# Seven-product feed-forward units: weight blocks and sums paired in another way, and the second weight chunk loaded into another buffer

## The chip, the core and the metric

One core of a Trainium2 chip runs the whole program, two layers of an encoder in float32. The metric is the device time of one execution in microseconds (us); lower is better. TensorE multiplies, VectorE (DVE) and ScalarE (ACT) do the elementwise work, GpSimd (POOL) does almost nothing here, and SyncE's queue (SP) issues nearly all loads and stores.

## What is computed

Each layer projects the normed input, runs two groups of heads (retention and differential attention), adds the projected result to `x`, and ends with a gated feed-forward part. Only that last part is touched:

```python
h = rms_norm(x, ffn_norm_g[l])
x = x + (jax.nn.silu(h @ w_gate[l]) * (h @ w_up[l])) @ w_down[l]
```

`x` is 512 rows of 1024, `w_gate` and `w_up` are 1024 x 2816, `w_down` is 2816 x 1024, and there are two layers.

## The kernel before, in words

**Precision.** Every float32 operand of a product is split into a high part, rounded to the matmul's float32r type, and a low part, the rest. A product is three matmuls: high x high, high x low, low x high. A split is one ScalarE cast (`hi`) and one VectorE subtraction (`lo`).

**Feed-forward part.** The 2816 inner columns are cut into 22 blocks of 128 (`ff`), taken in four groups: `FFN = [(0, 4), (4, 12), (12, 18), (18, 22)]`. After the blocks of a group, the group's part of the down projection is added to `x`. The first group (`gate_up`) is plain: two products per block, of full depth. The other three groups, 18 blocks a layer and 36 in all, are computed by `seven` (L726 to L773). It takes gate and up together as a 2 x 2 block product: the depth of 1024 is cut in two halves (g1, g2 of the gate weight, u1, u2 of the up weight), the 512 rows of `x` in two halves, and seven products of a Strassen kind stand for eight. The combinations on the side of `x` are made once a layer (`combine`, L695 to L716, during the first group and after it) and stay in memory as high and low parts. On the weights' side each unit makes four sums: s3 = u1 - g1, s1 = u1 - u2, s2 = g1 - s1, s4 = g2 - s2 (L730 to L733, 128 x 512 each).

**A unit's weights.** The host lays them out as two chunks of 128 x 1024: `a` = (g1, u2) and `b` = (g2, u1). Both are loaded into the tag `raw` (three buffers; L727, with the issue in `load_piece`, L168). The sums s31 = (s3, s1) and s24 = (s2, s4) lie in the tag `ah` (three buffers; the attention uses it earlier). `split_in` (L718 to L721) splits `a` into one buffer pair `hi`/`lo`, of which there are three (`NHL`), and `s31` into another one. The same three pairs serve every other weight chunk of the kernel, among them the down projection's (`split_chunk`, L192 and L196). s2 and s4 are split apart into four buffers of the tag `mix` (`split`, L220 and L221), and g2 into two of the tag `rn`; in the last group s24 is split as one into two buffers of tag `h`, and g2 goes to tag `w`.

**A unit's products.** `product` (L747 to L751) issues 12 matmuls of 256 columns: four depth tiles, three matmuls each. In the order of the program: g1 into bank `pa` (tag `acc`), a ScalarE copy of `pa` into `g` (L756); s2 added onto `pa`, copied into `g` (L759); s1 into `pc` (tag `o`); s3 added onto `pa`, copied into `u` (L762) and summed with `pc` on VectorE (L763); g2 into `pb` (tag `sc`), added to `g` (L765); u2 added onto `pa`; then the next unit's preparation and its g1; then s4 added onto `pc`, summed into `g` (L769), the Silu, two multiplications (L771, L772) and the split of the result for the down projection. So s2 waits for the copy of g1's result, s3 for the copy of s2's, u2 for the copy of s3's, and s4 for L763. Each of the three bank tags has two banks.

**Order of the work.** The program's order is a priority, no more: the kernel is written with a tile framework that orders each engine's instructions, when the program is built, by a simulated timeline (`schedule_with_timeline_sim=True`), and hands buffers of a tag to the tiles that ask for them. So the order on an engine departs from the program's where an operand was not ready in that timeline. Once built, each engine runs its list in order; a wait holds what is behind it. The generators `seven` are advanced by L787 to L792: first step (preparation and g1) of a unit, middle step (s2 to u2), first step of the next, last step (s4 and the end).

**Down projection.** Its weight chunks are loaded by L800 into `raw`, split by L192 and L196, multiplied by L203 to L205 (512 columns) and added to `x` by L631.

Of the kernel before, what the change touches and what calls it, by code (L numbers as in the profile page):

```python
# [8 lines left out]
F32 = mybir.dt.float32  # L9
F32R = mybir.dt.float32r  # L10
AF = mybir.ActivationFunctionType
ALU = mybir.AluOpType

P = 128
D = 1024
T = 512
DEPTH = 2
# [5 lines left out]
FT = DFF // P  # L23
# [10 lines left out]
FFN = [(0, 4), (4, 12), (12, 18), (18, FT)]  # L34
PLAIN = FFN[0][1]
# [4 lines left out]
NW, NQK, NMIX, NAH, NHL = 12, 11, 20, 3, 3  # L40
# [14 lines left out]
def encoder_kernel(ctx: ExitStack, tc: tile.TileContext, xT, wfirst, wsingle, wvv, wout, wgu, wdn, prm, lam, cst, outT):  # L55
    nc = tc.nc
# [4 lines left out]
    tpool = ctx.enter_context(tc.tile_pool(name="tpool", bufs=1))  # L61
# [5 lines left out]
    def nm(s):  # L67
        uid[0] += 1
        return f"{s}{uid[0]}"

    def big(s, dt=F32, tag="w", bufs=NW):
        return tpool.tile([P, T], dt, tag=tag, name=nm(s), bufs=bufs)
# [19 lines left out]
    def f32(ap):  # L92
        return ap.bitcast(F32)
# [68 lines left out]
    def new_chunk(n, pieces=1):  # L162
        return wpool.tile([P, 1024], F32, tag="raw", name=nm("raw"), bufs=3), n, pieces

    def load_piece(new, src, i):
        raw, n, pieces = new
        s = slice(i * n // pieces, (i + 1) * n // pieces)
        nc.sync.dma_start(raw[:, s], src[:, s])  # L168

    def load_chunk(src, n=1024, pieces=1):  # L170
        new = new_chunk(n, pieces)
        for i in range(pieces):
            load_piece(new, src, i)
        return new

    def parts():
        return tuple(wpool.tile([P, 1024], F32R, tag=t, name=nm(t), bufs=NHL) for t in ("hi", "lo"))
# [40 lines left out]
    def split(src, tag, bufs):  # L218
        hi, lo = pair() if tag == "h" else [big(n, F32R, tag, bufs) for n in ("hi", "lo")]
        nc.scalar.copy(hi, src)  # L220
        nc.vector.tensor_tensor(lo, src, f32(hi), op=ALU.subtract)  # L221
        return hi, lo
# [84 lines left out]
    def layer(l, n1, h, x_src, first_raw):  # L307
# [28 lines left out]
        mix = [None] * 8  # L336
# [378 lines left out]
                )  # L715
            )  # L716

        def split_in(raw, hi, lo, n=1024):  # L718
            nc.scalar.copy(hi, raw[:, :n])  # L719
            nc.vector.tensor_tensor(lo, raw[:, :n], f32(hi), op=ALU.subtract)  # L720
            return [(hi[:, i * T : (i + 1) * T], lo[:, i * T : (i + 1) * T]) for i in range(n // T)]  # L721

        def wide():
            return tpool.tile([P, 1024], F32R, tag="h", name=nm("s24"), bufs=8)

        def seven(ff, act, tag, bufs):  # L726
            a, b = load_chunk(wgu[l, ff, 0])[0], load_chunk(wgu[l, ff, 1])[0]  # L727
            s31, s24 = (tpool.tile([P, 1024], F32, tag="ah", name=nm("s"), bufs=NAH) for _ in range(2))
            u1 = b[:, T:]
            nc.vector.tensor_tensor(s31[:, :T], u1, a[:, :T], op=ALU.subtract)  # L730
            nc.vector.tensor_tensor(s31[:, T:], u1, a[:, T:], op=ALU.subtract)
            nc.vector.tensor_tensor(s24[:, :T], a[:, :T], s31[:, T:], op=ALU.subtract)
            nc.vector.tensor_tensor(s24[:, T:], b[:, :T], s24[:, :T], op=ALU.subtract)  # L733

            late = ff >= FFN[-1][0]
            g1, u2 = split_in(a, *parts())
            tag2 = ("w", NW) if late else ("rn", 4)
            if late:
                s2, s4 = split_in(s24, wide(), wide())
            else:  # L740
                s2, s4 = (split(s24[:, i * T : (i + 1) * T], "mix", NMIX) for i in range(2))
            s3, s1 = split_in(s31, *parts())
            (g2,) = split_in(b, big("g2h", F32R, *tag2), big("g2l", F32R, *tag2), T)

            pa, pb, pc = (bank() for bank in (acc_bank, sc_bank, out_bank))

            def product(ps, w, r, start):  # L747
                for k in range(4):
                    L, R = cut(w, slice(None), slice(k * P, (k + 1) * P)), comb[k][r]
                    for i, (x1, x2) in enumerate(((0, 0), (0, 1), (1, 0))):  # L750
                        nc.tensor.matmul(ps[:, :C], L[x1], R[x2], start=start and k + i == 0, stop=k == 3 and i == 2, skip_group_check=True)  # L751


            g, u = big("g"), big("u")
            product(pa, g1, "b11", True)
            nc.scalar.copy(g[:, H1], pa[:, :C])  # L756
            yield
            product(pa, s2, "t2", False)
            nc.scalar.copy(g[:, H2], pa[:, :C])  # L759
            product(pc, s1, "t1", True)  # L760
            product(pa, s3, "t3", False)
            nc.scalar.copy(u[:, H2], pa[:, :C])  # L762
            nc.vector.tensor_tensor(u[:, H2], pc[:, :C], u[:, H2], op=ALU.add)  # L763
            product(pb, g2, "b21", True)
            nc.vector.tensor_tensor(g[:, H1], pb[:, :C], g[:, H1], op=ALU.add)  # L765
            product(pa, u2, "t4", False)
            yield
            product(pc, s4, "b22", False)
            nc.vector.tensor_tensor(g[:, H2], pc[:, :C], g[:, H2], op=ALU.add)  # L769
            func(g, g, AF.Silu)  # L770
            nc.vector.tensor_tensor(u[:, H1], pa[:, :C], g[:, H1], op=ALU.mult)  # L771
            nc.vector.tensor_tensor(u[:, H2], u[:, H2], g[:, H2], op=ALU.mult)  # L772
            act.append(split(u, tag, bufs))  # L773

        for a0, a1 in FFN:
# [6 lines left out]
            else:  # L782
                units = []
                for ff in range(a0, a1):
                    tag = ("h", 8) if not last else ("mix", NMIX) if ff < a0 + 2 else ("rn", 4)
# [7 lines left out]
            n = (a1 - a0) * P  # L793
            for m in range(KT):
# [7 lines left out]
                w = cut(ww, slice(None), slice(m % 2 * n, (m % 2 + 1) * n)) if both else ww  # L802
# [23 lines left out]
    n, h, raws = Norm(), [], []  # L826
# [7 lines left out]
    for l in range(DEPTH):  # L834
        if l:
            raws = [load_chunk(wfirst[l, c]) for c in range(4)]
        n, h = layer(l, n, h, xT if l == 0 else xscr, raws)
# [16 lines left out]
def _layout(inputs):  # L854
    import numpy as np

    f = {k: np.asarray(v) for k, v in inputs.items()}
    a = {}
    a["xT"] = f["x"].reshape(T, D).T.reshape(KT, P, T)
    w = f["w_in"].reshape(DEPTH, KT, P, 3584).transpose(0, 2, 1, 3)  # L860
    cols = {"rq": 0, "rk": 512, "rv": 1024, "rg": 1536, "dq": 2048, "dk": 2560, "dv": 3072}

    def sel(n, f, width):
        return w[:, :, :, cols[n] + f : cols[n] + f + width]

    g = np.concatenate([sel(n, m * P, P) for n, m in FIRST], 3)
    a["wfirst"] = g.reshape(DEPTH, P, 4, 1024).transpose(0, 2, 1, 3)
    a["wsingle"] = np.stack([sel(n, m * P, P).reshape(DEPTH, P, 1024) for n, m in SINGLE], 1)
    a["wvv"] = np.stack(
        [  # L870
            np.stack([sel(n, 256 * i, 256).reshape(DEPTH, P, 2, 1024).transpose(0, 2, 1, 3) for i in range(2)], 1)
            for n in ("rv", "dv")
        ],
        1,
    )
    w = f["w_out"].reshape(DEPTH, 2, 4, P, 4, 256)[:, ::-1]
    a["wout"] = w.transpose(0, 1, 4, 3, 2, 5).reshape(DEPTH, 2, 4, P, 1024)
    g = f["w_gate"].reshape(DEPTH, KT, P, FT, P).transpose(0, 3, 2, 1, 4).reshape(DEPTH, FT, 1, P, 1024)
    u = f["w_up"].reshape(DEPTH, KT, P, FT, P).transpose(0, 3, 2, 1, 4).reshape(DEPTH, FT, 1, P, 1024)

    g, u = (t[:, :, 0].reshape(DEPTH, FT, P, 2, 512) for t in (g, u))
    gu = np.stack([g, u], 2)
    mixed = np.stack([np.stack([g[..., 0, :], u[..., 1, :]], 3), np.stack([g[..., 1, :], u[..., 0, :]], 3)], 2)
    a["wgu"] = np.concatenate([gu[:, :PLAIN], mixed[:, PLAIN:]], 1).reshape(DEPTH, FT, 2, P, 1024)
    w = f["w_down"].reshape(DEPTH, FT, P, KT, P)
    a["wdn"] = w.transpose(0, 3, 2, 1, 4).reshape(DEPTH, KT, P, FT * P)

    def col(v):
        return v.reshape(DEPTH, KT, P).transpose(2, 0, 1).reshape(P, DEPTH * KT)

    def twice(v):
        return np.concatenate([v, v], 1).T

    dec = np.stack([f["ret_decay_fwd"], f["ret_decay_bwd"]], 1)
    pair = np.repeat(dec.reshape(DEPTH * 2 * 4, 2).T, HD, 0)
    lam = np.stack([f["lambda_q1"], f["lambda_k1"], f["lambda_q2"], f["lambda_k2"]], 1)
    a["prm"] = np.concatenate(
        [
            col(f["attn_norm_g"]),
            col(f["ffn_norm_g"]),  # L900
            twice(f["ret_norm_g"]),
            twice(f["dq_norm_g"]),
            twice(f["dk_norm_g"]),
            f["diff_norm_g"].T,
            np.tile(dec.reshape(1, -1), (P, 1)),
            pair,
        ],
        1,
    )
    a["lam"] = np.tile(lam.reshape(1, -1), (P, 1))  # L910
    a["cst"] = _constants()
    return {k: np.ascontiguousarray(v) for k, v in a.items()}
# [15 lines left out]
```

## Time and profile before

| | us |
|---|---|
| median of three runs | 1271.79 (1269.89 to 1272.04) |
| the profiled execution | 1271.07 |
| its span, first to last instruction | 1268.9 |
| TensorE busy | 1246.7 |
| VectorE busy | 959.7 |
| ScalarE busy | 680.2 |

The page and the views come from the one profiled execution. A line of a group of instructions gives: source line, engine, operation, tiles written <- tiles read, shape, count, busy time in us and mean ns of one, and after the second bar the engine's idle time before them with what ended it. In a timeline the columns are start (us from the span's start), duration, engine, line, operation, tiles, shape and, in brackets, the engine's idle time before it and its releaser. Matmuls are pipelined: a row of 0.28 us is followed by the next 0.12 us later, and the ends are modelled. TensorE's granted clock was full in nearly all of the span.

### The profile page before, as it was taken

The page shows a single profiled execution, that of the slowest core. Times are in us where ns is not written, and L with a number is a line of the kernel's source. Part 1 is how long each engine was busy: PE and PEld are TensorE (multiplying, and loading weights), DVE is VectorE, ACT ScalarE, POOL GpSimd, SP SyncE. Part 2 cuts the span into 40 slices and gives each one's busy share as a digit, 9 for nine tenths or more (in the row PEclk, how much of TensorE's full clock was granted, in tenths as well). Part 3 has the DMA queues.
Part 4 walks back from the last instruction along what each step waited for, and adds up shares of the span by engine and source line. Part 5 has one row for each costly group of instructions (what it writes and reads, how often), then busy time and mean ns, then how long its engine had stood idle before and what let it go on. Part 6 is the DMA issues. An engine that isn't in the chain of part 4 may idle for free.

```text
span 1268.9 us, 19110 instructions
## 1 busy us (share of the span) xinstructions
PE 1246.7 (98%) x7516; PEld 1097.9 (87%) x7516; DVE 959.7 (76%) x1614; ACT 680.2 (54%) x1134; POOL 17.9 (1%) x42
## 2 busy tenths in 40 slices
PE   9999999999999999999999999999999999999988
PEld 8888988768899989989888889987788998898887
DVE  6899769858988567757478997698789885675664
ACT  6778657445455334434458786564554553254341
POOL 1000000000000000000000000000000000000000
PEclk9999999999999999999999999999999999999999
DMA  7212223113233242242252122141232332322322
GB/s 264 89 60 67 67 67 134 50 59 107 69 132 100 84 133 84 70 130 84 93 173 84 50 83 67 52 150 51 67 100 83 131 103 70 130 96 64 125 85 82
DMA packets 39258, 120.17 MB, mean 95 GB/s; under 512 B 4480, under 2 KB 4736, under 8 KB 39040
## 3 DMA queue, kind: packets, MB, share of 16 engines
q1 hardware_dynamic: 38736, 118.51, 28.6%
q8 instruction: 59, 0.97, 0.3%
q10 hardware_dynamic: 432, 0.44, 0.1%
q14 instruction: 31, 0.25, 0.1%
HBM read 114.74 MB, written 4.19 MB: 94 GB/s over the span
## 4 chain that ended last, share of the span: by engine, by line
PE 92%; DVE 4%; ACT 2%; issue 1%; DMA 1%; ACTq 0%; SPq 0%
PE acc L751 16%; PE acc L203 11%; PE acc L205 11%; PE acc L204 11%; PE o L751 8%; PE o L205 4%; PE o L203 4%; PE o L204 4%; PE sc L751 4%; PE sc L203 4%; PE sc L205 4%; PE sc L204 4%; PE sc L397 2%; PE o L498 1%; PE sc L482 1%; ACT hi L719 1%
## 5 line engine op out<-in xcount | busy, mean ns | idle before, releaser
L192 ACT CAST hi<-raw 128x1024 fp32r<-128x1024 f32 (+2 forms) x139 | 138.1, 1001 | 169.1 <-PE acc L204 59.4
L196 DVE TENSOR_TENSOR lo<-raw,hi 128x1024 fp32r<-128x1024 f32 (+2 forms) x140 | 161.6, 1158 | 53.1 <-ACT hi L192 52.6
L203 PE MATMUL acc<-h,hi 128*128 128x512 f32 x404 | 159.0, 395 | 0.6 <-ACT hi L192 0.6
L204 PE MATMUL acc<-h,hi 128*128 128x512 f32 x404 | 158.2, 392 | 0.0
L205 PE MATMUL acc<-h,lo 128*128 128x512 f32 x404 | 158.0, 392 | 0.0
L751 PE MATMUL acc<-hi,hi 128*128 128x256 f32 x400 | 113.7, 284 | 0.0
L751 PE MATMUL acc<-lo,hi 128*128 128x256 f32 x400 | 113.1, 283 | 0.0
L751 PE MATMUL acc<-hi,lo 128*128 128x256 f32 x400 | 113.0, 283 | 0.0
L203 PEld LDWEIGHTS acc<-h,hi 128*128 128x128 f32 x404 | 75.8, 188 | 17.5 <-ACT hi L192 1.9
L205 PEld LDWEIGHTS acc<-h,lo 128*128 128x128 f32 x404 | 75.9, 188 | 15.8
L204 PEld LDWEIGHTS acc<-h,hi 128*128 128x128 f32 x404 | 75.9, 188 | 15.0
L751 PEld LDWEIGHTS acc<-hi,hi 128*128 128x128 f32 x400 | 76.5, 191 | 0.7 <-ACT u L762 0.2
L751 PEld LDWEIGHTS acc<-lo,hi 128*128 128x128 f32 x400 | 76.6, 191 | 0.3
L751 PEld LDWEIGHTS acc<-hi,lo 128*128 128x128 f32 x400 | 76.6, 191 | 0.0
L220 ACT CAST hi<-s 128x512 fp32r<-128x512 f32 x56 | 34.8, 621 | 62.6 <-PE o L751 32.9
L720 DVE TENSOR_TENSOR lo<-s,hi 128x1024 fp32r<-128x1024 f32 x36 | 43.9, 1220 | 27.5 <-ACT hi L719 27.5
L205 PE MATMUL sc<-h,lo 128*128 128x512 f32 x164 | 63.6, 390 | 0.0
L204 PE MATMUL sc<-h,hi 128*128 128x512 f32 x164 | 63.6, 390 | 0.0
L203 PE MATMUL sc<-h,hi 128*128 128x512 f32 x164 | 63.1, 392 | 0.3 <-ACT hi L192 0.3
L719 ACT CAST hi<-s 128x1024 fp32r<-128x1024 f32 x36 | 37.7, 1047 | 41.7 <-PE acc L751 38.3
L719 ACT CAST hi<-raw 128x1024 fp32r<-128x1024 f32 x36 | 37.8, 1050 | 39.6 <-PE acc L751 22.2
L106 ACT ACTIVATE sc<-sc,mx 128x512 f32<-128x512 f32 x64 | 46.0, 719 | 18.3 <-DVE mx L401 17.9
(243 smaller groups left out, 3577.5 us busy)
## 6 DMA issues: line engine op xcount, KB each, us to landing
raw<-in_wgu SPq DMA_DIRECT2D x88, 512.0 KB, 3.6
raw<-in_wsingle SPq DMA_DIRECT2D x32, 512.0 KB, 3.5
raw<-in_wvv SPq DMA_DIRECT2D x16, 512.0 KB, 3.8
raw<-in_wout SPq DMA_DIRECT2D x16, 512.0 KB, 3.7
raw<-in_wdn SPq DMA_DIRECT2D x32, 256.0 KB, 3.0
raw<-in_wdn SPq DMA_DIRECT2D x16, 512.0 KB, 3.9
raw<-in_wdn SPq DMA_DIRECT2D x16, 384.0 KB, 3.5
x<-in_xT SPq DMA_DIRECT2D x15, 256.0 KB, 5.5
```

Source lines behind the costliest of these rows:

```text
L106: i = nc.scalar.activation(out, src, f, **kw).ins
L192: c = nc.scalar.copy(hi[:, s], raw[:, s])
L196: nc.vector.tensor_tensor(lo[:, s], raw[:, s], f32(hi[:, s]), op=ALU.subtract)
L203: nc.tensor.matmul(out, L[0], R[0], start=start, stop=False)
L204: nc.tensor.matmul(out, L[0], R[1], start=False, stop=False)
L205: nc.tensor.matmul(out, L[1], R[0], start=False, stop=stop)
L220: nc.scalar.copy(hi, src)
L397: nc.tensor.matmul(ps, q[m][:, t], k[m][part], start=part == 0, stop=part == 1)
L482: nc.tensor.matmul(out, ks[hh][part][:, sb], qs[hh][:, tb], start=part == 0, stop=part == 1)
L719: nc.scalar.copy(hi, raw[:, :n])
L720: nc.vector.tensor_tensor(lo, raw[:, :n], f32(hi), op=ALU.subtract)
L751: nc.tensor.matmul(ps[:, :C], L[x1], R[x2], start=start and k + i == 0, stop=k == 3 and i == 2, skip_group_check=True)
```

## The change

The host lays the four weight blocks out by depth halves: `a` = (g1, u1) and `b` = (g2, u2), where it was (g1, u2) and (g2, u1).

`a` is still loaded into `raw`. `b` is loaded into a buffer of `ah`, straight by a load on the SP queue, where it was a `raw` buffer. The sums s3 and s1 are made as before, u1 being now in `a`. s2 is written over u1 in `a`, once both sums that read u1 are made, so that `a` becomes (g1, s2). s4 gets a buffer of 128 x 512 in `w`; the tile s24 is gone.

All three wide tiles are split into `hi`/`lo` pairs: `a` as (g1, s2), `s31` as (s3, s1), `b` as (g2, u2). s4 alone is split into `mix` (in the last group into `w`). So a unit takes three of the `hi`/`lo` pairs where it took two, one `raw` buffer where it took two, and two `ah` buffers as before, one for a load and one for a sum where both held sums. It uses two buffers of `mix` where it used four, and none of `rn` (in the last group none of `h`). The products, their operands' values, their order in the program and everything behind them stay as they were.

```diff
--- before.py
+++ after.py
@@ -715,32 +715,28 @@
                 )
             )
 
-        def split_in(raw, hi, lo, n=1024):
-            nc.scalar.copy(hi, raw[:, :n])
-            nc.vector.tensor_tensor(lo, raw[:, :n], f32(hi), op=ALU.subtract)
-            return [(hi[:, i * T : (i + 1) * T], lo[:, i * T : (i + 1) * T]) for i in range(n // T)]
-
-        def wide():
-            return tpool.tile([P, 1024], F32R, tag="h", name=nm("s24"), bufs=8)
+        def split_in(raw):
+            hi, lo = parts()
+            nc.scalar.copy(hi, raw)
+            nc.vector.tensor_tensor(lo, raw, f32(hi), op=ALU.subtract)
+            return [(hi[:, i * T : (i + 1) * T], lo[:, i * T : (i + 1) * T]) for i in range(2)]
+
+        def four(s):
+            return tpool.tile([P, 1024], F32, tag="ah", name=nm(s), bufs=NAH)
 
         def seven(ff, act, tag, bufs):
-            a, b = load_chunk(wgu[l, ff, 0])[0], load_chunk(wgu[l, ff, 1])[0]
-            s31, s24 = (tpool.tile([P, 1024], F32, tag="ah", name=nm("s"), bufs=NAH) for _ in range(2))
-            u1 = b[:, T:]
-            nc.vector.tensor_tensor(s31[:, :T], u1, a[:, :T], op=ALU.subtract)
-            nc.vector.tensor_tensor(s31[:, T:], u1, a[:, T:], op=ALU.subtract)
-            nc.vector.tensor_tensor(s24[:, :T], a[:, :T], s31[:, T:], op=ALU.subtract)
-            nc.vector.tensor_tensor(s24[:, T:], b[:, :T], s24[:, :T], op=ALU.subtract)
-
-            late = ff >= FFN[-1][0]
-            g1, u2 = split_in(a, *parts())
-            tag2 = ("w", NW) if late else ("rn", 4)
-            if late:
-                s2, s4 = split_in(s24, wide(), wide())
-            else:
-                s2, s4 = (split(s24[:, i * T : (i + 1) * T], "mix", NMIX) for i in range(2))
-            s3, s1 = split_in(s31, *parts())
-            (g2,) = split_in(b, big("g2h", F32R, *tag2), big("g2l", F32R, *tag2), T)
+
+            a, b, s31 = load_chunk(wgu[l, ff, 0])[0], four("b"), four("s")
+            nc.sync.dma_start(b, wgu[l, ff, 1])
+            s4 = big("s4")
+            nc.vector.tensor_tensor(s31[:, T:], a[:, T:], b[:, T:], op=ALU.subtract)
+            nc.vector.tensor_tensor(s31[:, :T], a[:, T:], a[:, :T], op=ALU.subtract)
+            nc.vector.tensor_tensor(a[:, T:], a[:, :T], s31[:, T:], op=ALU.subtract)
+            g1, s2 = split_in(a)
+            s3, s1 = split_in(s31)
+            nc.vector.tensor_tensor(s4, b[:, :T], a[:, T:], op=ALU.subtract)
+            g2, u2 = split_in(b)
+            s4 = split(s4, *(("w", NW) if ff >= FFN[-1][0] else ("mix", NMIX)))
 
             pa, pb, pc = (bank() for bank in (acc_bank, sc_bank, out_bank))
 
@@ -878,10 +874,9 @@
     g = f["w_gate"].reshape(DEPTH, KT, P, FT, P).transpose(0, 3, 2, 1, 4).reshape(DEPTH, FT, 1, P, 1024)
     u = f["w_up"].reshape(DEPTH, KT, P, FT, P).transpose(0, 3, 2, 1, 4).reshape(DEPTH, FT, 1, P, 1024)
 
-    g, u = (t[:, :, 0].reshape(DEPTH, FT, P, 2, 512) for t in (g, u))
-    gu = np.stack([g, u], 2)
-    mixed = np.stack([np.stack([g[..., 0, :], u[..., 1, :]], 3), np.stack([g[..., 1, :], u[..., 0, :]], 3)], 2)
-    a["wgu"] = np.concatenate([gu[:, :PLAIN], mixed[:, PLAIN:]], 1).reshape(DEPTH, FT, 2, P, 1024)
+    gu = np.concatenate([g, u], 2)
+    halves = gu.reshape(DEPTH, FT, 2, P, 2, 512).transpose(0, 1, 4, 3, 2, 5).reshape(gu.shape)
+    a["wgu"] = np.concatenate([gu[:, :PLAIN], halves[:, PLAIN:]], 1)
     w = f["w_down"].reshape(DEPTH, FT, P, KT, P)
     a["wdn"] = w.transpose(0, 3, 2, 1, 4).reshape(DEPTH, KT, P, FT * P)
 
```

## Rows read from the trace of the kernel before

**Rows 1.** The page: its first line, busy time of each engine, and the chain that ended last by engine.

```profile
span 1268.9 us, 19110 instructions
...
PE 1246.7 (98%) x7516; PEld 1097.9 (87%) x7516; DVE 959.7 (76%) x1614; ACT 680.2 (54%) x1134; POOL 17.9 (1%) x42
...
PE 92%; DVE 4%; ACT 2%; issue 1%; DMA 1%; ACTq 0%; SPq 0%
```

**Rows 2.** Busy time by stretch, layer 0: the second, third and fourth feed-forward group (units of seven products: first, third and fifth row) and the down projections behind them. Here and in the prediction these groups of units are called the first, the second and the third (last) group of units. Columns as in the header line, (x) is the number of instructions.

```profile
core 0: us, PE busy (x) PEld busy (x) DVE busy (x) ACT busy (x) POOL busy (x), PEclk, DMA share, GB/s
349.00:437.00 88.00, 87.99 (x701) 86.25 (x700) 71.20 (x117) 45.52 (x77) 0.00 (x0) 1.00 0.32 108
437.00:474.00 37.00, 37.00 (x165) 30.49 (x164) 21.44 (x30) 10.70 (x13) 0.00 (x0) 1.00 0.39 123
474.00:543.00 69.00, 66.64 (x526) 64.64 (x525) 47.48 (x77) 32.52 (x56) 0.00 (x0) 1.00 0.24 78
543.00:572.00 29.00, 29.00 (x126) 23.21 (x125) 18.26 (x26) 8.99 (x11) 0.00 (x0) 1.00 0.43 132
572.00:622.00 50.00, 46.78 (x362) 45.15 (x362) 31.57 (x48) 21.12 (x33) 1.57 (x3) 1.00 0.27 85
```

**Rows 3.** What TensorE waited for in the whole span, longest first in total: us in total, number of waits, the longest. L751 stands in the first line and in no other.

```profile
PE o L751 <- ACT hi L719: 12.0, 14, 1.1
PE o L203 <- DVE sq L513: 2.2, 1, 2.2
PE sc L397 <- DVE mx L401: 1.5, 4, 0.5
PE aux L117 <- DVE eps_sb L159: 1.5, 1, 1.5
PE acc L203 <- ACT hi L192: 0.6, 2, 0.3
```

**Rows 4.** Timeline of TensorE and then of ScalarE around one of these waits, in the last group of layer 0.

```profile
591.88 0.28 PE L751 MATMUL acc<-lo,hi 128*128 128x256 f32 x1
592.00 0.28 PE L751 MATMUL acc<-hi,lo 128*128 128x256 f32 x1
593.35 0.39 PE L751 MATMUL o<-hi,hi 128*128 128x256 f32 x1 [1.07 <-ACT hi L719]
593.58 0.28 PE L751 MATMUL o<-lo,hi 128*128 128x256 f32 x1
593.70 0.32 PE L751 MATMUL acc<-hi,hi 128*128 128x256 f32 x1
...
592.25 1.04 ACT L719 CAST hi<-s 128x1024 fp32r<-128x1024 f32 x1 [2.92 <-PE acc L751]
593.21 0.37 ACT L762 COPY u<-acc 128x256 f32<-128x256 f32 x1
```

**Rows 5.** Groups of instructions by line and shape, whole span: VectorE, then ScalarE. A cast or low part of 1024 columns, the same of 512, and one of the four subtractions.

```profile
L720 DVE TENSOR_TENSOR lo<-s,hi 128x1024 fp32r<-128x1024 f32 x36 | 43.9, 1220 | 27.5 <-ACT hi L719 27.5
L221 DVE TENSOR_TENSOR lo<-s,hi 128x512 fp32r<-128x512 f32 x56 | 38.3, 686 | 6.1 <-ACT hi L220 3.5 <-PE o L751 1.7
L730 DVE TENSOR_TENSOR s<-raw,raw 128x512 f32<-128x512 f32 x36 | 24.8, 690 | 25.3 <-DMA raw<-in_wgu 20.0 <-issue 5.1
L732 DVE TENSOR_TENSOR s<-raw,s 128x512 f32<-128x512 f32 x36 | 24.6, 682 | 0.1
...
L719 ACT CAST hi<-raw 128x1024 fp32r<-128x1024 f32 x36 | 37.8, 1050 | 39.6 <-PE acc L751 22.2 <-PE o L204 11.2 <-PE sc L204 6.0
L220 ACT CAST hi<-s 128x512 fp32r<-128x512 f32 x56 | 34.8, 621 | 62.6 <-PE o L751 32.9 <-PE acc L751 14.4 <-DVE s L732 7.3
```

**Rows 6.** The stretch ahead of the first group of units in layer 0 (columns as in group 2), and TensorE's timeline at the two places where a product of that group is the first to wait, one in each layer.

```profile
324.00:344.00 20.00, 19.77 (x88) 16.04 (x86) 19.45 (x39) 9.62 (x16) 0.00 (x0) 1.00 0.16 54
...
344.20 0.39 PE L751 MATMUL o<-hi,hi 128*128 128x256 f32 x1 [0.43 <-ACT hi L719]
...
971.19 0.39 PE L751 MATMUL o<-hi,hi 128*128 128x256 f32 x1 [0.43 <-ACT hi L719]
```

**Rows 7.** Timeline at the beginning of the second group of units in layer 0: VectorE's first subtraction for its first unit, and TensorE's first product.

```profile
458.82 0.69 DVE L730 TENSOR_TENSOR s<-raw,raw 128x512 f32<-128x512 f32 x1 [3.52 <-DMA raw<-in_wgu]
...
474.32 0.28 PE L751 MATMUL acc<-bh,hi 128*128 128x256 f32 x1
```

**Rows 8.** Loads by line: count, size, median us from issue to landing; and what the SP queue waited for, whole span: us in total, number of waits, the longest.

```profile
raw<-in_wgu SPq DMA_DIRECT2D x88, 512.0 KB, 3.6
...
SPq L168 <- DVE lo L720: 114.8, 24, 9.6
SPq L168 <- DVE s L733: 77.7, 22, 10.6
```

**Rows 9.** What ScalarE waited for in the second group of units of layer 0 (474 to 546 us): its first line.

```profile
ACT hi L719 <- PE acc L751: 12.4, 7, 3.9
```

**Rows 10.** Busy time in four stretches of 10 us of the first group of units in layer 0 (columns as in group 2).

```profile
374.00:384.00 10.00, 10.00 (x85) 9.99 (x84) 9.15 (x16) 4.93 (x8) 0.00 (x0) 1.00 0.30 105
384.00:394.00 10.00, 10.00 (x84) 9.85 (x84) 9.02 (x16) 5.84 (x10) 0.00 (x0) 1.00 0.34 107
394.00:404.00 10.00, 9.99 (x82) 9.62 (x81) 8.53 (x16) 5.99 (x10) 0.00 (x0) 1.00 0.32 107
404.00:414.00 10.00, 10.00 (x85) 10.00 (x85) 8.82 (x16) 5.74 (x11) 0.00 (x0) 1.00 0.31 105
```

## The prediction, made before the changed kernel ran

> **What bounds the kernel now.** I read the page first: TensorE is busy 1246.7 of 1268.9 us and holds 92% of the chain that ended last [rows 1]. So the work of ScalarE, VectorE and the queues counts only where TensorE waits for it, and all the idle time there is to win is 22.2 us. Next the table by stretches, for the three groups of seven-product units of layer 0 with the down projections between them [rows 2]: TensorE's idle time lies in the second and third group (2.36 and 3.22 us), not in the first (0.01), and not in the down projections before them. Then what TensorE waited for: of its idle time, 12.0 us in 14 waits stand under one name, the product into bank `o` that waits for ScalarE's cast at L719 [rows 3]. That is product s1, waiting for the high part of `s31`. No wait for VectorE, a load or a copy stands at L751.
>
> The stretch around one such wait shows why [rows 4]. The last matmul of s3 starts at 592.00. The cast of the next unit's `s31` starts at 592.25, released by that product: its source had been ready, but the three `hi`/`lo` buffers were held by the running unit's (g1,u2) and (s3,s1) and the next unit's (g1,u2). It takes 1.04 us, and TensorE resumes at 593.35. Behind the cast stands the copy of bank `acc` into `u` (593.21), for which u2 waits (593.70). In a product matmuls start 0.12 us apart, so 593.35 - 592.00 - 0.12 = 1.23 us are lost, where the view says 1.07: a modelled matmul end hides 0.16 of each wait. The 14 waits cost 12.0 + 14 x 0.16 = 14.2 us.
>
> **The change, part by part.** A unit is 7 products of 12 matmuls, 84 x 0.12 = 10.08 us; the program's order is g1, s2, s1, s3, g2, u2, s4, with the next unit's g1 ahead of s4.
>
> *Pairing by time of use.* (g1,u2) is held from the first product to the sixth, and this long hold uses up the ring. Afterwards (g1,s2), (s3,s1), (g2,u2) are each let go after two neighbouring products. There are three pairs a unit instead of two, on three buffers, but each is free again five products (7.2 us) before the next unit needs it, and a split takes 1.05 + 1.22 us [rows 5], 2.3 with no queue. Two things follow at the place of the wait. The cast of the next `s31` may still wait for s3, as now; but g2 now comes out of the last pair, is not run ahead as filler, and is available just then, with the next unit's g1 (split since s2) behind it. So I take the 14.2 us as gone but for the two waits at the beginning of the first groups (344.20 and its like in layer 1). There VectorE is busy 19.45 of 20 us [rows 6] and the new order has it do the same work; they stay, 2 x (0.43 + 0.16) = 1.2 us. Term: -13.0.
>
> *What is late next: the copies.* In three places a unit, a freed pair lets a cast of 1.05 us start just when a copy out of bank `acc` is due. From the last matmul of s3 to u2 went 593.70 - 592.00 = 1.70 us, with the cast ahead of the copy [rows 4]. One product in between covers 12 x 0.12 + 0.12 = 1.56 and leaves 0.14; two cover all; none leaves 1.58. After s2 and after s3 a product waits for the copy; after u2 the next g1 uses another bank. That is 72 handovers in 36 units, each between 0 and 0.14 with cover: 0 to 10.1 us. I take one in five, 2.0, since the same cast precedes the copy in the first group now, where TensorE idles for 0.01 us [rows 2]. Term: +2.0.
>
> *Fewer instructions.* 28 units (all but the last groups') did two 512-wide splits for s2 and s4 and one for g2, and now do one 1024-wide and one 512-wide. VectorE saves 2 x 0.686 - 1.220 = 0.15 us a unit, ScalarE 2 x 0.621 - 1.050 = 0.19 [rows 5]. The eight last-group units keep their count. The four subtractions stay four of 0.68 us. All this is hidden: no wait of TensorE names VectorE at L751 [rows 3]. Term: 0; were VectorE the bound, 28 x 0.15 = 4.3 us would come off. The Trainium skill (Perfetto Trace Analysis, section Per-engine timelines) says that operations of ScalarE and VectorE carry a fixed cost per instruction, so that fewer and wider ones are faster; 0.15 and 0.19 us are that cost here. By that rule the sum would be 4.3 us lower, by the rows it is not, because VectorE's time is covered.
>
> *First product later in its data.* g1 shared its split with u2, straight from the load; now the split needs both loads and three subtractions. At the beginning of group 2 these ran from 458.82 on, and the first product started at 474.32 [rows 7]. From the landing to g1 the new order needs 3 x 0.69 + 1.05 + 1.22 = 4.3 us, and there were 15.5: 11 us of cover. If that cover went, a group's beginning would cost up to 4.3 us, six times 26; I take 0.
>
> *Second load into the sums' tag.* The load of `b` leaves the three `raw` buffers and goes into `ah`, where `s31` and `s24` were; `s4` moves to `w`. Two loads a unit are still issued on the SP queue in the same order, 3.6 us each to landing [rows 8], and behind each stand the next unit's loads and the down projection's. `raw` now has one load a unit, so SP's waits for `raw` (114.8 us behind L720, 77.7 behind L733 [rows 8]) become shorter. What it costs instead: `b` waits for an `ah` buffer, which the split of an earlier `s31` or `b` frees. With three buffers the load of unit i+2 can go when the split of unit i's `b` is done, after u2 of unit i-1: over 17 us ahead of its own first product, of which load, subtractions and split need 3.6 + 2.1 + 2.3 = 8.0. Term: 0.
>
> **Sum.** The profiled execution took 1271.07 us, its span 1268.9, and 2.2 lie around it; the median of three is 0.7 above it. 1271.07 - 13.0 + 2.0 = 1260.1; I predict 1260.0. A difference of 0.2% (2.5 us) is about the least that a measurement of this kernel can tell from none.
>
> **The rivals.**
> *A, the wait moves to the copies* (0.14). Three casts a unit rather than two start from a buffer's release, on an engine whose casts at L719 already waited 12.4 us for TensorE in the second group [rows 9], and the copies stand behind them. If all 72 handovers cost 0.14: 1271.07 - 13.0 + 10.1 = 1268.2; if one in ten finds no product as cover instead, 7 x 1.58 = 11 and 1269. For it: the cast went ahead of the copy at 592.25. Against it: the first group. The Trainium skill (TensorE: Matmul & The Clock Gate, "Architectural detail") says that ScalarE and VectorE take their instructions strictly first in, first out; the rows agree, a ready copy did not pass the cast.
>
> *B, slower: the loads of `b` turn over too late* (0.13). If sums take two of the three `ah` buffers, one is left for `b`, and unit closes on unit: cast and low part of `b` 2.3 after u2, load 3.6, three subtractions 2.1 (all in one queue), cast and low part 2.3: 10.3 us against 10.08 of products. It decides from the point where a load of `b` is issued less than 8 us ahead of its own g1. VectorE, busy 8.5 to 9.2 us of 10 in the steady first group [rows 10], would add queueing to five of the steps. At 1 us in each of the 30 units that follow another in a group: 1271.07 - 13.0 + 30 = 1288. For it: `b` is held until the last split, twice as long as a sum was. Against it: three buffers, and a sum is held only from its subtraction to its split.
>
> *C, nothing changes* (0.07). `s31`'s cast still begins when s3 ends, and TensorE's order, fixed at build time by a scheduler, could leave s1 right behind it as now. Then the 14 waits stay: 1271. Against it: g2 and g1 are free to stand there.
>
> **How the numbers follow.** Forecast 0.66, between 1256.9 (all 14.2 gone, nothing new) and 1266. With the runs' scatter below the profiled execution (1.2) the low end is 1255. The high end takes in A, to 1270; B and C are left out, 0.20 together. Faster by over 0.2% (below 1269.2): the forecast and half of A, 0.73. Within 0.2%: C and part of A, 0.12. Slower: B and what A could grow to, 0.15.
>
> **What would show it.** Right: the waits of the `o` product for the cast of `s31` fall from 14 to two or so; the second and third group's stretches become some 2 and 3 us shorter a layer; any new wait of TensorE at the products is short and names a copy (`g` or `u` out of `acc`); ScalarE and VectorE have 28 instructions fewer each; SP's waits for `raw` shrink. Wrong: the same 1.1 us waits for the cast after s3 (C); many waits on copies that add up to 10 us (A); TensorE waiting at g1 for a cast or a low part with VectorE idle before its subtraction until a load of `b` lands (B); or idle time at the beginning of the groups, which would say that the cover of 11 us was not there.

## The result, and the profile after

The changed kernel takes 1263.99 us (median, 1262.17 to 1264.42) where the kernel before, beside it on the same chip, takes 1271.67: a ratio of 0.994, interval 0.9922 to 0.9957. It is faster by 7.7 us; forecast were 1260.0 us in a range of 1255 to 1270.

The page of the profiled execution (1264.3 us); first its span, the engines' busy times, and the chain that ended last:

```profile
span 1262.5 us, 19030 instructions
...
PE 1249.1 (99%) x7516; PEld 1099.3 (87%) x7516; DVE 957.8 (76%) x1586; ACT 673.8 (53%) x1106; POOL 17.9 (1%) x42
...
PE 96%; ACT 2%; DVE 1%; issue 0%; ACTq 0%
```

VectorE and ScalarE issue 28 instructions fewer each [rows 1]. What TensorE waited for, at the products (L747 is now their line, L720 the 1024-wide cast, L755 the copy of s2's result): us in total, number, longest.

```profile
PE o L747 <- ACT hi L720: 1.9, 2, 1.0
...
PE acc L747 <- ACT g L755: 0.9, 2, 0.5
```

Of the 14 waits for the cast of s31 [rows 3] two are left, but each of these is 0.96 us and not 0.43 [rows 6]; and two waits for a copy are new. Busy time in the stretches of [rows 2] and [rows 6] that hold units (the work stands a little later in them now):

```profile
349.00:437.00 88.00, 87.40 (x687) 84.82 (x686) 70.94 (x109) 43.58 (x69) 0.00 (x0) 1.00 0.33 103
474.00:543.00 69.00, 68.86 (x535) 66.62 (x535) 49.99 (x78) 32.58 (x52) 0.00 (x0) 1.00 0.27 83
572.00:622.00 50.00, 50.00 (x377) 48.06 (x377) 33.35 (x52) 24.84 (x37) 1.56 (x3) 1.00 0.27 85
324.00:344.00 20.00, 20.00 (x90) 16.57 (x89) 18.72 (x36) 8.85 (x16) 0.00 (x0) 1.00 0.25 80
```

The idle time of the second and third group is gone (2.36 and 3.22 us before, 0.14 and 0.00 now), and the first group, which had 0.01, has 0.60. The same place as in [rows 4], the last group of layer 0, TensorE and then ScalarE:

```profile
598.85 0.28 PE L747 MATMUL acc<-hi,lo 128*128 128x256 f32 x1
598.97 0.28 PE L747 MATMUL sc<-bh,lo 128*128 128x256 f32 x1
...
600.05 0.28 PE L747 MATMUL sc<-bh,lo 128*128 128x256 f32 x1
600.21 0.39 PE L747 MATMUL o<-hi,hi 128*128 128x256 f32 x1
600.44 0.28 PE L747 MATMUL o<-lo,hi 128*128 128x256 f32 x1
600.56 0.30 PE L747 MATMUL acc<-hi,hi 128*128 128x256 f32 x1
...
599.11 1.05 ACT L720 CAST hi<-s 128x1024 fp32r<-128x1024 f32 x1 [1.12 <-PE acc L747]
600.07 0.36 ACT L758 COPY u<-acc 128x256 f32<-128x256 f32 x1
```

The cast still begins when s3 ends (598.85), and the copy still stands behind it: from s3 to u2 it takes 1.71 us, as it took 1.70. But ten matmuls of g2 (bank `sc`) and two of the next s1 now run in that time.

**What the idle view leaves out.** Waits of a tenth of a microsecond barely show in it. So I also add up, over the matmuls of `product`, what lies between a matmul's start and the start of the one before above the usual 0.12 us (0.23 behind a 512-column matmul). This loss, worked out from each profiled trace, stands in the table by group of units, both layers together; "elsewhere" is the same sum over all other matmuls. The last column is VectorE's waits for loads of the units' weights (us, number).

| kernel | median us | ratio to before (interval) | first | second | third | products in all | elsewhere | load waits |
|---|---|---|---|---|---|---|---|---|
| before | 1271.67 | 1 | 2.8 | 7.7 | 8.1 | 18.6 | 38.5 | 20.0, 16 |
| changed | 1263.99 | 0.9940 (0.9922 to 0.9957) | 7.4 | 2.8 | 0.9 | 11.1 | 39.7 | 6.9, 4 |
| pair_raw | 1270.19 | 0.9989 (0.9980 to 0.9999) | 12.2 | 2.4 | 3.6 | 18.2 | 39.7 | 59.9, 39 |
| load_only | 1273.68 | 1.0015 (1.0007 to 1.0024) | 8.2 | 5.4 | 3.3 | 17.0 | 43.6 | 4.7, 4 |
| before_copy | 1268.54 | 0.9977 (0.9969 to 0.9986) | 5.9 | 2.4 | 4.3 | 12.5 | 42.5 | 19.2, 23 |
| after_halves | 1264.65 | 0.9946 (0.9934 to 0.9958) | 4.6 | 3.7 | 3.2 | 11.6 | 39.7 | 6.1, 4 |
| after_again | 1263.35 | 0.9939 (0.9927 to 0.9952) | 7.4 | 2.8 | 0.9 | 11.1 | 37.3 | 6.1, 4 |
| after_copy | 1258.22 | 0.9901 (0.9887 to 0.9914) | 4.8 | 0.5 | 0.5 | 5.8 | 38.8 | 5.2, 4 |
| after_copy_u | 1258.62 | 0.9894 (0.9879 to 0.9909) | 5.1 | 1.1 | 0.7 | 6.9 | 39.0 | 5.2, 4 |
| after_s1 | 1265.81 | 0.9959 (0.9945 to 0.9972) | 5.5 | 3.3 | 1.4 | 10.2 | 40.1 | 5.6, 4 |
| after_copy_s1 | 1258.51 | 0.9901 (0.9888 to 0.9915) | 2.3 | 0.5 | 0.5 | 3.4 | 41.4 | 9.9, 4 |
| pair_raw_copy | 1272.74 | 1.0005 (0.9996 to 1.0014) | 11.8 | 5.1 | 2.9 | 19.8 | 39.8 | 64.2, 51 |
| swap_load | 1255.65 | 0.9877 (0.9863 to 0.9890) | 2.7 | 0.8 | 0.7 | 4.2 | 37.9 | 6.1, 4 |
| both_ah | 1266.43 | 0.9964 (0.9950 to 0.9977) | 10.5 | 1.9 | 1.0 | 13.4 | 37.8 | 38.6, 23 |

Each ratio is to the kernel before run beside that kernel on the same chip. The sums agree with the spans: products and elsewhere together fall by 6.3 us from before to changed, the spans by 6.4. "Elsewhere" also moves by itself: two profiled executions of the changed kernel, "changed" and "after_again", differ by 2.4 us, nearly all of it in the first 20 us of the program (4.9 and 2.8 us lost there), and alike at the products.

### The profile page after: what moved, and what is told of

Same layout as the page of the kernel before. It is cut to its first block, busy times and chain, and to the rows that moved or that the text cites. A ratio compares the mean times of both kernels' runs of the same rounds, so it can differ in the third digit from the quotient of the medians.

```text
span 1262.5 us, 19030 instructions
## 1 busy us (share of the span) xinstructions
PE 1249.1 (99%) x7516; PEld 1099.3 (87%) x7516; DVE 957.8 (76%) x1586; ACT 673.8 (53%) x1106; POOL 17.9 (1%) x42
## 4 chain that ended last, share of the span: by engine, by line
PE 96%; ACT 2%; DVE 1%; issue 0%; ACTq 0%
PE acc L747 17%; PE acc L203 11%; PE acc L204 11%; PE acc L205 11%; PE o L747 8%; PE o L203 4%; PE o L205 4%; PE o L204 4%; PE sc L203 4%; PE sc L205 4%; PE sc L204 4%; PE sc L747 4%; PE sc L397 2%; PE o L498 1%; PE sc L482 1%; PE aux L413 1%
## 5 line engine op out<-in xcount | busy, mean ns | idle before, releaser
L747 PE MATMUL acc<-hi,hi 128*128 128x256 f32 x432 | 123.9, 287 | 1.5 <-ACT g L755 0.9
L747 PE MATMUL acc<-lo,hi 128*128 128x256 f32 x432 | 122.1, 283 | 0.0
L747 PE MATMUL acc<-hi,lo 128*128 128x256 f32 x432 | 122.1, 283 | 0.0
L747 PEld LDWEIGHTS acc<-hi,hi 128*128 128x128 f32 x432 | 82.5, 191 | 3.8 <-ACT g L755 2.7
L747 PEld LDWEIGHTS acc<-lo,hi 128*128 128x128 f32 x432 | 82.6, 191 | 0.5
L747 PEld LDWEIGHTS acc<-hi,lo 128*128 128x128 f32 x432 | 82.6, 191 | 0.0
L720 ACT CAST hi<-raw 128x1024 fp32r<-128x1024 f32 x36 | 37.7, 1048 | 65.8 <-PE acc L747 45.4
L721 DVE TENSOR_TENSOR lo<-raw,hi 128x1024 fp32r<-128x1024 f32 x36 | 44.1, 1225 | 35.4 <-ACT hi L720 34.8
L720 ACT CAST hi<-b 128x1024 fp32r<-128x1024 f32 x36 | 37.9, 1052 | 49.3 <-ACT g L752 12.4
L720 ACT CAST hi<-s 128x1024 fp32r<-128x1024 f32 x36 | 37.8, 1051 | 48.9 <-PE acc L747 34.3
```

What stands on the lines that cost most here:

```text
L720: nc.scalar.copy(hi, raw)
L721: nc.vector.tensor_tensor(lo, raw, f32(hi), op=ALU.subtract)
```

## The experiments

**The pairing alone, and the load alone.** `pair_raw` is the changed kernel with one edit:

```diff
-            a, b, s31 = load_chunk(wgu[l, ff, 0])[0], four("b"), four("s")
-            nc.sync.dma_start(b, wgu[l, ff, 1])
+            a, b, s31 = load_chunk(wgu[l, ff, 0])[0], load_chunk(wgu[l, ff, 1])[0], four("s")
```

> The changed kernel, but with `b` loaded into `raw` as before; the new pairing alone. Theory T (the pairs are held for two neighbouring products instead of up to six, so the ring of three always has a next product's operands in it): all of the gain, 1262 to 1266 us, and at most four waits of the products for the cast of s31. Rival L (it is the load of `b` in its own place, not the pairing, that lets the casts come earlier): no gain, 1269 to 1273, with some 14 waits of 1.1 us.

`load_only` is the kernel before with `b` in `ah`, and s2 and s4 in tiles of their own:

```diff
-            a, b = load_chunk(wgu[l, ff, 0])[0], load_chunk(wgu[l, ff, 1])[0]
-            s31, s24 = (tpool.tile([P, 1024], F32, tag="ah", name=nm("s"), bufs=NAH) for _ in range(2))
+            a = load_chunk(wgu[l, ff, 0])[0]
+            b, s31 = (tpool.tile([P, 1024], F32, tag="ah", name=nm(n), bufs=NAH) for n in ("b", "s"))
+            nc.sync.dma_start(b, wgu[l, ff, 1])
+            s2, s4 = big("s2"), big("s4")
...
+            s2, s4 = (split(t, *(("h", 8) if late else ("mix", NMIX))) for t in (s2, s4))
```

> The kernel before, with its pairing (g1,u2), (g2,u1) and its two-of-three pairs a unit, but with `b` loaded into the tag `ah` (s2 and s4 get tiles of their own instead of s24); the load's new place alone. T: no gain or a small one, 1268 to 1273 us, since (g1,u2) still holds a pair from the first product to the sixth; s1 still waits for the cast of s31 in the second and third group. Rival L: 1262 to 1266 and the waits gone.

Alone, the pairing is worth 1.7 us (the interval of its ratio reaches to 0.9999) and the load costs 1.8; together they are worth 7.7. Both theories missed the pairing: T's time, since it gains next to nothing, and L's reason, since the waits for s31 are gone there. What TensorE and VectorE waited for in `pair_raw` (whole span), and the third group's worst place, VectorE, SP and TensorE (L721 low part, L731 and L732 subtractions, L746 products):

```profile
PE acc L746 <- DVE lo L721: 5.4, 5, 2.2
```

```profile
DVE s L732 <- DMA raw<-in_wgu: 31.8, 17, 3.7
DVE s L731 <- DMA raw<-in_wgu: 28.1, 22, 2.2
```

```profile
576.47 1.22 DVE L721 TENSOR_TENSOR lo<-raw,hi 128x1024 fp32r<-128x1024 f32 x1
581.23 0.69 DVE L732 TENSOR_TENSOR s<-raw 128x512 f32<-128x512 f32 x1 [3.55 <-DMA raw<-in_wgu]
581.84 1.22 DVE L721 TENSOR_TENSOR lo<-raw,hi 128x1024 fp32r<-128x1024 f32 x1
...
577.71 0.33 SPq L168 DMA_DIRECT2D raw<-in_wgu  x1
...
581.04 0.28 PE L746 MATMUL acc<-hi,lo 128*128 128x256 f32 x1
583.11 0.39 PE L746 MATMUL acc<-bh,lo 128*128 128x256 f32 x1 [1.79 <-DVE lo L721]
```

The low part that ends at 577.69 frees a `raw` buffer, and 0.02 us later the load is issued; VectorE comes to that unit's subtraction, waits 3.55 us for the data, and holds the low part behind it, for which TensorE waits. This is the prediction's rival B, with its place changed: the loads turn over too late in `raw`, not in `ah`. In `load_only` 10 of the 14 waits for s31 are gone too; waits for copies and for the cast of g2 stand in their place, and the down projections lose more (43.6 elsewhere):

```profile
PE acc L750 <- ACT g L758: 4.3, 10, 1.0
PE o L750 <- ACT hi L719: 3.3, 4, 1.0
PE sc L750 <- ACT g2h L719: 2.8, 5, 0.8
```

**The order on ScalarE, in the kernel before.** `before_copy` only puts the next unit's s31 cast behind the running unit's copy into `u`:

```diff
-            nc.scalar.copy(hi, raw[:, :n])
+            c = nc.scalar.copy(hi, raw[:, :n])
+            if behind in copies:
+                tc.add_manual_dep(c.ins, copies[behind], order, reason="copies first")
...
+            s3, s1 = split_in(s31, *parts(), behind="u")
...
+            copies["u"] = nc.scalar.copy(u[:, H2], pa[:, :C]).ins.name
```

> The kernel before, with its pairing and loads; only the order of two ScalarE instructions is set: the cast of the next unit's s31 stands behind the running unit's copy of `acc` into `u`. Then u2 of the running unit no longer waits behind that cast, and can be TensorE's filler while the cast runs. Rival O (what cost the time was not how long the pairs are held but that the cast stood ahead of the copy, so that nothing but s1 was left to run): most of the gain, 1262 to 1266 us. T: the copy takes 0.4 us and delays the cast; u2 gives 1.44 us of cover for the 1.04 us cast, so part of the gain, but g2 has been spent earlier and in each unit the copy itself stands bare (about 0.6 us): 1266 to 1271.

3.3 us less, in T's range and outside rival O's: the waits for s31 fall from 14 to two, and ten waits for a copy, 0.44 us on the mean, stand in their place:

```profile
PE acc L755 <- ACT u L766: 4.4, 10, 0.5
...
PE o L755 <- ACT hi L721: 0.9, 2, 0.4
```

So the whole change, either half of it, and an order on ScalarE each remove most or all of that wait. What they are worth is decided by where the time returns.

**Fewer instructions.** `after_halves` casts and subtracts `b` in two halves:

```diff
-            g2, u2 = split_in(b)
+            bh, bl = parts()
+            for s in (slice(0, T), slice(T, 2 * T)):
+                nc.scalar.copy(bh[:, s], b[:, s])
+                nc.vector.tensor_tensor(bl[:, s], b[:, s], f32(bh[:, s]), op=ALU.subtract)
+            g2, u2 = [(bh[:, i * T : (i + 1) * T], bl[:, i * T : (i + 1) * T]) for i in range(2)]
```

> The changed kernel, with the split of `b` in two 512-wide halves: 36 more casts on ScalarE and 36 more subtractions on VectorE than it has, 8 more than before on each. T and the prediction's step (fewer instructions are worth nothing, the time is covered): 1263 to 1265 us, no change against the changed kernel. Rival I (the fixed cost of the instructions is on the path): VectorE 36 x 0.15 = 5.4 us and ScalarE 36 x 0.19 = 6.8 us longer, so 1268 to 1270.

1264.65 us, within the expectation of no change, with VectorE at 960.2 us busy and ScalarE at 680.0, the work of the kernel before [rows 1]. Rival I's 5.4 to 6.8 us are not there, so the saved instructions are no visible part of the gain. The total hides a trade, though: by the table the first group loses 2.8 us less than in the changed kernel and the other two 3.2 more, among it four waits of a g1 for its own cast, one at the beginning of each of these groups:

```profile
482.79 0.39 PE L751 MATMUL acc<-bh,hi 128*128 128x256 f32 x1 [1.06 <-ACT hi L720]
```

The Trainium skill's fixed cost per instruction (Perfetto Trace Analysis, section Per-engine timelines) is there: for 36 more instructions each, VectorE's busy time rises by 2.4 us and ScalarE's by 6.2, on engines that have room for it.

**The copies, in the changed kernel.** These ran beside the changed kernel itself, `after_copy_u` alone later and on another chip; it is compared by its ratio to the kernel before.

> The changed kernel again, unchanged, as the measure for the three edits that run beside it on the same chip: 1262 to 1265 us.

`after_copy` orders both casts behind the copies, with the edit of `before_copy` and:

```diff
-            g1, s2 = split_in(a)
-            s3, s1 = split_in(s31)
+            g1, s2 = split_in(a, "g")
+            s3, s1 = split_in(s31, "u")
...
+            copies["g"] = nc.scalar.copy(g[:, H2], pa[:, :C]).ins.name
```

> The changed kernel, with the cast of (g1,s2) ordered behind the running unit's copy of `acc` into `g`, and the cast of s31 behind its copy into `u`, on ScalarE. It tests the prediction's step on the copies. If the short losses at the products (0.08 to 0.14 us each, 5.5 us in all after the change) are the copies standing behind the casts: some 3 us less, 1260 to 1262. If they are what a TensorE that waits for any semaphore loses at a handover: no change, 1263 to 1265.

`after_copy_u` does so for s31 alone.

> The changed kernel, with only the cast of s31 ordered behind the running unit's copy of `acc` into `u`; the cast of (g1,s2) stands where it did. If the loss at the copies lies at u2 alone (the place that the trace of before showed): as with both orders, 1258 to 1259 us. If both copies carry it in equal parts: 1260 to 1262.

`after_copy` takes 5.1 us less than the changed kernel beside it, more than the 3 expected; with s31's order alone the ratio is the same within its interval (0.9894 and 0.9901). A place of such a loss in the changed kernel, first group, TensorE and ScalarE:

```profile
396.37 0.28 PE L747 MATMUL acc<-hi,lo 128*128 128x256 f32 x1
...
397.57 0.28 PE L747 MATMUL sc<-bh,lo 128*128 128x256 f32 x1
397.99 0.39 PE L747 MATMUL acc<-hi,hi 128*128 128x256 f32 x1
398.21 0.28 PE L747 MATMUL acc<-lo,hi 128*128 128x256 f32 x1
...
396.62 1.05 ACT L720 CAST hi<-raw 128x1024 fp32r<-128x1024 f32 x1 [3.87 <-PE acc L747]
397.57 0.37 ACT L755 COPY g<-acc 128x256 f32<-128x256 f32 x1
```

s2 ends, the cast of the next `a` goes first, the copy second, and only ten matmuls of g2 cover them, since two had been run ahead: 397.99 - 397.57 - 0.12 = 0.30 us lost, and 0.10 more at the next matmul. At the opening of the first group no cast stands ahead of the copy, but nothing covers it either: s3 stands right behind s2 (VectorE, ScalarE, TensorE):

```profile
353.88 1.22 DVE L721 TENSOR_TENSOR lo<-b,hi 128x1024 fp32r<-128x1024 f32 x1
...
355.18 0.37 ACT L755 COPY g<-acc 128x256 f32<-128x256 f32 x1 [2.50 <-PE acc L747]
...
354.87 0.28 PE L747 MATMUL acc<-hi,lo 128*128 128x256 f32 x1
355.61 0.39 PE L747 MATMUL acc<-hi,hi 128*128 128x256 f32 x1 [0.46 <-ACT g L755]
```

A third kind of loss is no copy. The next unit's g1 starts 0.06 us after VectorE's multiplication that reads a bank `acc` (L767) has ended, 0.12 us late:

```profile
399.17 0.41 DVE L767 TENSOR_TENSOR u<-acc,g 128x256 f32<-128x256 f32 x1
...
399.40 0.28 PE L747 MATMUL acc<-hi,lo 128*128 128x256 f32 x1
399.64 0.39 PE L747 MATMUL acc<-bh,hi 128*128 128x256 f32 x1
```

In `after_copy` the copy of the same kind goes at once and the casts follow it:

```profile
394.47 0.37 ACT L759 COPY g<-acc 128x256 f32<-128x256 f32 x1 [2.14 <-PE acc L751]
394.73 0.63 ACT L106 ACTIVATE g<-g 128x512 f32<-128x512 f32 x1
395.27 1.04 ACT L722 CAST hi<-raw 128x1024 fp32r<-128x1024 f32 x1
...
398.55 0.37 ACT L762 COPY u<-acc 128x256 f32<-128x256 f32 x1 [1.72 <-PE acc L751]
398.81 1.05 ACT L722 CAST hi<-s 128x1024 fp32r<-128x1024 f32 x1
```

The edit sets ScalarE's order, and the build-time order of TensorE's products moves with it, so the 5.1 us are the price of the order as a whole, not of the copies' 0.37 us alone. `after_copy_u` shows it: it sets no order at the copy into `g`, and yet of the changed kernel's twelve waits for that copy only the bare one of layer 0's opening (0.62) is left.

**The first group's opening.** `after_s1` holds the first s1 behind its unit's g1 on TensorE; `after_copy_s1` has both edits.

```diff
+                        if behind and k + i == 0:
+                            tc.add_manual_dep(mm.ins, behind, order, reason="s1 behind g1")
...
-            product(pc, s1, "t1", True)
+            product(pc, s1, "t1", True, after_g1)
```

> The changed kernel, with the first matmul of s1 ordered behind its unit's g1 on TensorE. In the changed kernel the first unit's s1 begins inside the down projection, where it waits for the cast of s31 (1.1 us), and is then spent when s3 needs something to cover its copy (0.6 us). If these two places are what the first group of units lost by the change (4.5 us in both layers against the kernel before): 2 x (1.1 + 0.6) = 3.4 us less, 1260 to 1261. If the loss lies in VectorE's full queue there (combinations of the last depth tile and the splits of two units): the wait only moves to another product, 1263 to 1265.

> Both edits in one kernel. If both theories hold, their gains add: 1257 to 1259 us. If only one, as that one.

No gain, 1265.8 and 1258.5 us. At the opening of the changed kernel s1 waits 0.96 us inside the down projection, because its cast (344.39) stands behind three others on ScalarE; in `after_s1` s1 is out of the way, and the down projection's own matmul waits longer for VectorE's low part. The changed kernel, TensorE and ScalarE, then `after_s1`, TensorE:

```profile
345.49 0.39 PE L747 MATMUL o<-hi,hi 128*128 128x256 f32 x1 [0.96 <-ACT hi L720]
...
342.62 0.40 ACT L707 CAST b<-b 128x256 fp32r<-128x256 f32 x1
342.93 0.61 ACT L220 CAST hi<-ta 128x512 fp32r<-128x512 f32 x1
343.45 1.05 ACT L720 CAST hi<-raw 128x1024 fp32r<-128x1024 f32 x1
344.39 1.04 ACT L720 CAST hi<-s 128x1024 fp32r<-128x1024 f32 x1
```

```profile
343.64 0.50 PE L205 MATMUL o<-hi,lo 128*128 128x512 f32 x1 [1.47 <-DVE lo L196]
```

The products lose 1.9 us less in the first group (7.4 to 5.5) and the rest of the program more. The wait moved, as the second theory said (its range ended at 1265), to the engine that is full there [rows 6].

**Which load, and how many.** `swap_load` exchanges the two places, `pair_raw_copy` puts the copies' order into `pair_raw`, and `both_ah` mirrors `pair_raw`:

```diff
+            a = four("a")
+            nc.sync.dma_start(a, wgu[l, ff, 0])
+            b, s31 = load_chunk(wgu[l, ff, 1])[0], four("s")
...
+            a, b, s31 = four("a"), four("b"), new_chunk(1024)[0]
+            nc.sync.dma_start(a, wgu[l, ff, 0])
+            nc.sync.dma_start(b, wgu[l, ff, 1])
```

> The changed kernel, with the two loads' places exchanged: `a` into the tag `ah`, `b` into `raw`. Theory R, formed from the run with both loads in `raw` (1270 us, the load of `b` landing late): it is the count that decides, two loads a unit turning over in three `raw` buffers once the pairing holds them longer; which of the two goes to `ah` does not matter: 1262 to 1266 us. Rival: it is `b` in `raw` that is late, because `b` waits for its split behind that of s31, whatever else lies in `raw`: 1268 to 1271.

> Both loads in `raw` (the new pairing alone), and the two casts ordered behind the running unit's copies. Theory R says that the late load is a loss of its own, beside that of the copies: some 5 us less than the pairing alone, 1264 to 1266, and VectorE still waits for the load of `b`. Rival (the late load only came of casts that let the buffers go late behind the copies; one loss, not two): 1258 to 1260.

> The changed kernel's pairing, with both loads in the tag `ah` and s31 in `raw`: the mirror of the pairing alone. Theory R (two loads in one tag of three buffers: each turnover holds a load's 3.6 us to landing, two subtractions and a split): VectorE waits for the loads again and most of the gain is gone, 1267 to 1273 us. Rival S (what is late in `raw` is that the down projection's loads and a unit's two loads share it in turn, so that inside a group two loads in a tag of their own would do): 1256 to 1264 us, and VectorE waits for no load inside a group.

`both_ah` brings the waits for loads back, 38.6 us in 23 against 6.9 in 4, 18 of the 23 inside a group, so rival S is refuted. But theory R's price is too high: at 1266.4 (just below its range) some 5 of the 7.7 us of gain are left, where `pair_raw` keeps 1.7:

```profile
DVE raw L733 <- DMA b<-in_wgu: 23.1, 16, 3.7
DVE raw L734 <- DMA a<-in_wgu: 15.5, 7, 3.6
```

So two loads a unit in one tag of three buffers land late in either tag; that does not take the down projection's loads in `raw`. Why the late loads cost TensorE more in `raw` than in `ah` is not shown. `pair_raw_copy` refutes both expectations: the copies' order gains nothing there. VectorE's low parts are late for want of data, and TensorE waits for those in more places than without the order (18 waits, 8.6 us, against 5 and 5.4 in `pair_raw` at the same bank).

`swap_load` shows that which load moves is not neutral either: 1255.65 us, below theory R's range and the fastest of all, by the ratios 8 us under the changed kernel. Its products lose 4.2 us. The one line left for them:

```profile
PE o L748 <- ACT hi L720: 1.3, 2, 0.7
```

No edit here separates why. The traces show that its low part of `b` in the opening ends at 352.4, where that of the changed kernel ends at 355.1, and that the new bare copies there are gone:

```profile
351.15 1.22 DVE L721 TENSOR_TENSOR lo<-raw,hi 128x1024 fp32r<-128x1024 f32 x1
```

They also show another build-time order on TensorE. Here s2's last matmul (352.50) is followed by ten of g2 (352.62 to 353.69), not by s3. From the third unit of the first group on, the order of the products then repeats itself unit by unit to the last but one, while the changed kernel leaves it at the fifth of eight.

## Why the prediction was right, and where it was mis-sized

- **Pairing (-13.0).** The mechanism was right: the cast still starts behind s3, and g2 fills the time. From start to start the 14 waits cost 14.2 us; the two that stay cost 2.2, not 1.2, in part because a short cast (342.62, 0.40 us) now stands among those ahead of theirs. Measured: -12.0.
- **Copies (+2.0): the step that was mis-sized.** "One in five" at 0.14 us was taken from the cover of a whole product. Of the twelve waits for the copy into `g`, six have twelve matmuls as cover (0.06 lost). TensorE's list splits products, so four have only ten (0.30 lost at 397.99), and at the two openings of the first group there is none (0.62 lost at 355.61; the low part that g2 needs ends at 355.10, after s2's last matmul has started). Every wait costs 0.10 more at the second matmul. Losses below 0.4 us at the products rise from 4.4 to 7.6, and two of 0.62 are new: +4.4. By what released them, with the 0.10 behind each, the copies rise from 0.5 to 4.0 us: +3.5 where +2.0 was forecast. The other new part, which the prediction did not name, is g1 waiting for VectorE's multiplication, 0.4 to 2.2 us. Rival A was thus true in part; -12.0 + 4.4 = -7.6 is about the gain.
- **Fewer instructions (0).** In the total `after_halves` bears it out; its waits moved as well.
- **First product later in its data (0).** True: at the beginning of group 2 the low part of (g1,s2) ends at 468.7 and the first product starts at 477.22. The sign that was to speak against it, idle time at a group's beginning, does show in the first group, whose loss went from 2.8 to 7.4; but there too no g1 waits for its data (the first one starts at 350.68, 0.23 us behind the 512-column matmul before it), the waits name s31's cast and a copy.
- **Second load into the sums' tag (0).** As a price it held. As a reading it was wrong: the step was taken for neutral, and without it the pairing gains 1.7 us. So the gain rests on a part that the sum passed over; that the change had it was luck, as far as the sum goes. Rival B described that turnover and its waits, for the wrong tag. SP's waits at the loads into `raw` did shrink, 192.5 us [rows 8] to 65.9, but 157.7 us in 28 waits are new at the load of `b` into `ah`: they moved.
- **Rival C** is refuted: s1 no longer stands right behind s3.
- **The frame.** "All the idle time there is to win is 22.2 us" went by the idle view. By the starts, 18.6 us were lost at the products alone and 57.1 in all, and `swap_load` gains 16.

Open: why the load of `a` in `ah` is 8 us better than that of `b`, and what the first group's opening would cost with a less full VectorE; no run tried that. A fourth pair of `hi`/`lo` buffers, the direct test of the ring, was not tried either.

## What to carry to other kernels

A wait that stands under one name is easily removed, here by several edits; price the place where it returns, engine by engine, before booking the gain. A load's buffer comes free only when the last split out of it is done (577.69, and the next load goes out at 577.71), so where a change lets splits come later, count loads per buffer together with their landing time. Where an engine keeps its order, try the short instruction on which the busiest engine waits ahead of the long one that only prepares: it gained 3.3 us in the kernel before and 5.1 in the changed one, and nothing where the loads were late.

## What the runs showed of the hardware

At the products a wait of TensorE costs more than its idle time: the first 256-column matmul behind it is followed only 0.22 us later (397.99, 398.21; 345.49, 345.71), the others 0.12. In the changed kernel 52 losses of 0.08 to 0.14 us stand at the products. And two executions of the same program can differ by 2.1 us in the first 20 us alone (4.9 and 2.8 us lost), more than several of the edits tried here, so a span is compared stretch by stretch.
